# A LoRA update on one core: the first eight tiles as two parts, their stores behind VectorE's turn

## The chip, the cores and the metric

The kernel runs on one core of one Trainium2 chip. The metric is device time in microseconds of one execution; three executions of the kernel before gave a median of 123.61 us, from 123.61 to 123.78. The core has TensorE (PE in the profile), VectorE (DVE), ScalarE (ACT), GpSimd (POOL) and SyncE (SP). SyncE does no arithmetic; here it issues all transfers. They run on 16 DMA engines, which serve one queue.

## The reference

```python
batch, seq, d_model, r = 16, 512, 768, 16     # x: 16 x 512 x 768, all float32
lora = np.matmul(np.matmul(x, A), B)          # A: 768 x 16, B: 16 x 768
return (x + scale * lora).astype(np.float32)  # scale = 0.5
```

There are 8192 rows of x. About 25 MB are read and 25 MB written; the two products are small beside that.

## The kernel before, in words

**Tiles and parts.** A tile is 128 rows by 768 columns, 3,072 bytes on each of the 128 partitions of the on-chip memory; x is 64 tiles. `PARTS` (line 14) cuts them into stretches of rows. Within a part of S tiles, partition p holds S consecutive rows of x, so a transfer of the whole part reads or writes S x 3,072 bytes in one go on each partition. A transfer of only some of a part's tiles (`memory`, line 96) touches a piece of each of these stretches and steps over the rest. The buffer `x_sb` has room for all parts but the last; the last 16 tiles go into the slots of the first 16, once those are stored.

**Loads and stores.** `LOADS` (line 106) and `STORES` (line 128) list transfers as (part, first tile, tiles). Before the change the first part has 8 tiles. It is loaded as 2 and then 6 tiles, and stored as one transfer of 8. Each load has a semaphore of its own; the first two stores have `s_out0` and `s_out1`. A transfer's semaphore is full at 16.

**Groups.** Compute goes by 8 groups of 8 tiles. For each group ScalarE and GpSimd cast x to half precision (`narrowed`, line 186), VectorE transposes in blocks of 32 (`turned`, line 248), TensorE multiplies with A (`projected`, line 278) into `ps_yt`, ScalarE scales and spreads the result into `y_bd` (line 238), TensorE multiplies with B in four pairs of tiles (`raised`, line 293) into two PSUM buffers `lora_ps`, and VectorE adds each pair to x in place (`summed`, line 252). VectorE turns group g+1 before it adds group g.

**Order.** Every engine's program is written out by hand, with waits on semaphores. SyncE's (`on_sync`, line 135) is what the change touches most. It issues the first two loads, the small ones of A and B, four more loads, then waits: for the sums of groups 0 and 1 (line 144, where it also tells TensorE that a PSUM buffer is free), and then for `s_lora` to reach 10, which is TensorE's second pair of group 2 (line 169). Then it issues the stores of parts 0 and 1. When the first has landed it issues the first half of the last load, when the second has landed the second half. The three stores of 16 tiles follow, each when its groups are summed; the first of these also waits for `s_raise`, TensorE's start of group 5's product with B.

Of the kernel before, what the change touches and what calls it, by code (L numbers as in the profile page):

```python
# [10 lines left out]

PARTS = [8, 8, 16, 16, 16]


GROUP = 8
# [11 lines left out]
def kernel(  # L29
# [8 lines left out]
    nc = tc.nc  # L38
# [9 lines left out]
    NC = D // 64  # L48
    NG = sum(PARTS) // GROUP
    PAIRS = GROUP // 2  # L50
    assert sum(PARTS) * P == T and NG * GROUP == sum(PARTS)
    sc = float(scale)


    def sb(name, shape, dtype):
        return nc.alloc_sbuf_tensor(name, shape, dtype).ap()
# [3 lines left out]

    ROOM = sum(PARTS[:-1])
    x_all = sb("x_sb", [P, ROOM, D], fp32)
# [20 lines left out]
    def sem(name):  # L83
        sems.append(nc.alloc_semaphore(name))
        return sems[-1]
# [4 lines left out]
    tok = 0  # L90
    for i, S in enumerate(PARTS):
        parts.append(tok)
# [3 lines left out]
    def memory(t2, i, s, n):  # L96
        S = PARTS[i]
        return t2[ds(parts[i], S * P), :].rearrange("(p s) d -> p s d", s=S)[:, ds(s, n), :]

    def held(i, s, n):  # L100
        return tiles(where.index((i, s)), n)

    def tiles(t, n):
        return x_all[:, ds(t % ROOM, n), :]

    LOADS = [
        (0, 0, 2), (0, 2, 6), (1, 0, 8), (2, 0, 8), (2, 8, 8), (3, 0, 16), (4, 0, 8), (4, 8, 8)
    ]
    s_load = [sem(f"s_load{k}") for k in range(len(LOADS))]

# [8 lines left out]
    s_first, s_narrow, s_turned, s_taken = sem("s_first"), sem("s_narrow"), sem("s_turned"), sem("s_taken")  # L119
    s_y, s_spread, s_lora = sem("s_y"), sem("s_spread"), sem("s_lora")  # L120

    s_free = [sem(f"s_free{p}") for p in range(PAIRS)]
    s_out0, s_out1, s_raise = sem("s_out0"), sem("s_out1"), sem("s_raise")

    s_sum, s_out = sem("s_sum"), sem("s_out")

    MMS = 2 * NC
    STORES = [(0, 0, 8), (1, 0, 8), (2, 0, 16), (3, 0, 16), (4, 0, 16)]

    STORED = [where.index((i, s + n - 1)) // GROUP for i, s, n in STORES]  # L130

    section = ExitStack()
    section.enter_context(tc.tile_critical(no_gpsimd_drain=True))  # L133

    def on_sync(e):
        def load(k):
            ld = LOADS[k]
            e.dma_start(out=held(*ld), in_=memory(x2, *ld)).then_inc(s_load[k], 16)  # L138

        def summed(k):  # L140
            e.wait_ge(s_sum, k + 1)
            if STORED[k] + 1 < NG:

                e.sem_inc(s_free[PAIRS - 1], 1)

        def store(k, done):
            st = STORES[k]
            e.dma_start(out=memory(out2, *st), in_=held(*st)).then_inc(done, 16)

        load(0)  # L150
        load(1)
        e.wait_ge(s_ready, 1)
        blocks = A.rearrange("(c e) r -> c (e r)", e=64)
        for c in range(SETS):
            e.dma_start(
                out=a_rows[c : SET * SET : SET, :], in_=blocks[ds(c * SET, SET), :]
            ).then_inc(s_a, 16)
        e.wait_ge(s_brows, 1)
        e.dma_start(out=b_rows[0 : R * APART : APART, :], in_=B).then_inc(s_b, 16)
        for k in range(2, len(LOADS) - 2):  # L160
            load(k)

        for p in range(2, PAIRS):
            e.sem_inc(s_free[p], 1)
        summed(0)
        summed(1)


        e.wait_ge(s_lora, 2 * PAIRS + 2)
        store(0, s_out0)  # L170
        store(1, s_out1)
        e.wait_ge(s_out0, 16)
        load(len(LOADS) - 2)
        e.wait_ge(s_out1, 16)
        load(len(LOADS) - 1)
        for k in range(2, len(STORES)):
            summed(k)
            if k == 2:


                e.wait_ge(s_raise, 6)
            store(k, s_out)

    here = set()

# [55 lines left out]
    def on_vector(e):  # L241
        e.wait_ge(s_a, SETS * 16 + 1)
        e.transpose(  # L243
            out=a_t[0:Q].rearrange("i k r c -> i (k r) c"),
            in_=a_rows[0:Q].rearrange("c (i k r) -> c (k r) i", k=2, r=R),
        ).then_inc(s_ready, 1)

        def turned(first, n):
            ts = [v[:, ds(first, n), :].bitcast(fp32) for v in (xt, xn)]
            return e.transpose(out=ts[0], in_=ts[1])  # L250

        def summed(g, p):
            xs = tiles(g * GROUP + 2 * p, 2)
            e.wait_ge(s_lora, g * PAIRS + p + 1)
            ins = e.tensor_tensor(out=xs, in0=xs, in1=lora[p % 2], op=mybir.AluOpType.add)  # L255
            if p + 1 == PAIRS and g in STORED:
                ins.then_inc(s_sum, 1)
            elif g + 1 < NG or p + 2 < PAIRS:
                ins.then_inc(s_free[p], 1)

        for h in range(2):
            e.wait_ge(s_first, h + 1)
            ins = turned(h * SUB, SUB)
        ins.then_inc(s_turned, 1)
        for g in range(NG):
            if g + 1 < NG:
                e.wait_ge(s_y, g + 1)
                e.wait_ge(s_narrow, 2 * (g + 1))  # L268
                turned(0, GROUP).then_inc(s_turned, 1)
            for p in range(PAIRS):  # L270
                summed(g, p)

    def on_tensor(e):
# [58 lines left out]
        for p in range(PAIRS):  # L332
            raised(p)

    on_sync(nc.sync)
    on_gpsimd(nc.gpsimd)
    on_scalar(nc.scalar)
    on_vector(nc.vector)
    on_tensor(nc.tensor)

    nums = [s.num for s in sems]
    assert nums == list(range(nums[0], nums[0] + len(nums))) and sems[-2:] == [s_sum, s_out]

    nc.gpsimd.wait_ge(s_sum, len(STORED))
    nc.gpsimd.sem_clear(range(nums[0], s_sum.num))
    nc.gpsimd.wait_ge(s_out, (len(STORES) - 2) * 16)
    nc.gpsimd.sem_clear(range(s_sum.num, s_out.num + 1))
    section.close()

# [34 lines left out]
```

## Time and profile before

| What | Value |
| --- | --- |
| median of three runs | 123.61 us (123.61 to 123.78) |
| profiled execution, its own time | 123.76 us |
| its span, first to last instruction | 121.9 us |
| DMA queue busy | 96.8% of 16 engines' span |
| moved | 50.43 MB, mean 414 GB/s |
| VectorE busy | 81.7 us, 67% |
| TensorE, ScalarE, GpSimd busy | 41%, 31%, 23% |

The profile's page gives each engine's busy time and share of the span. Its groups of instructions have the line, the engine, the operation, what it writes and reads, the count, the busy time in us, the mean ns of one, then the idle time of the engine just before them and what ended it. The chain lists, from the last instruction backwards, what released what. A line of a timeline or of the chain begins with its start and its duration in us. SyncE's lines (SPq) show the time at which a transfer is issued, not when it moves; a timeline merges issues of one line into one entry from the first to the last. Besides these the trace has a record of every DMA packet with its start, duration and size; a packet here is one partition's row of a transfer, and each DMA engine takes 8 of the 128 rows. Packets of one engine follow each other without a break, so 16 series can be followed from start to end.

### The profile page before, as it was taken

What the parts mean: (1) busy time and instruction counts of PE and PEld (TensorE: products, weight loads), DVE (VectorE), ACT (ScalarE), POOL (GpSimd) and SP (SyncE); (2) the same over time, 40 slices, a digit from 0 to 9 for tenths busy, and PEclk for the clock granted to TensorE, in tenths of its full rate; (3) what the DMA queues carried; (4) which work ended last, traced back from release to release, by engine and by line L of the source; (5) the groups of instructions that cost most, each with busy time, mean ns of one, the idle gap of its engine ahead of it and who ended that gap; (6) DMA issues with size and microseconds to landing.
All of it is one profiled execution on the core that took longest, in us unless ns stands there. A gap on an engine that the chain in (4) does not pass through costs nothing.

```text
span 121.9 us, 885 instructions
## 1 busy us (share of the span) xinstructions
PE 50.5 (41%) x322; PEld 29.3 (24%) x322; DVE 81.7 (67%) x42; ACT 37.4 (31%) x43; POOL 28.4 (23%) x24
## 2 busy tenths in 40 slices
PE   0000239487457457647756714774674320000000
PEld 0000026244233233424424402442442110000000
DVE  0003850799999999999999959999995991000000
ACT  4003929444426402917230093643004000000000
POOL 7732638044026002607100090630000000000000
PEclk9999999999999999999999999999999985555555
DMA  3999999999997996999989999998998999899890
GB/s 67 421 429 429 443 443 403 451 435 419 476 516 339 435 516 298 460 403 443 443 363 460 427 427 468 451 484 387 419 500 387 403 516 403 371 516 419 355 516 0
DMA packets 1928, 50.43 MB, mean 414 GB/s; under 512 B 236, under 2 KB 236, under 8 KB 392
## 3 DMA queue, kind: packets, MB, share of 16 engines
q1 hardware_dynamic: 1928, 50.43, 96.8%
HBM read 25.26 MB, written 25.17 MB: 414 GB/s over the span
## 4 chain that ended last, share of the span: by engine, by line
DVE 33%; DMA 29%; PE 9%; ACT 6%; POOL 2%; issue 2%; SPq 0%; DVEq 0%
DVE x_sb L255 21%; DMA x_sb<-in_x_dram 20%; DVE xt L250 12%; DMA out_dram<-x_sb 9%; PE ps_yt L281 6%; ACT xn L194 3%; PE lora_ps L302 3%; ACT y_bd L238 2%; POOL xn L194 2%; SPq L138 0%; SPq L379 0%; DVEq L268 0%; SPq L133 0%
## 5 line engine op out<-in xcount | busy, mean ns | idle before, releaser
L255 DVE TENSOR_TENSOR x_sb<-x_sb,lora_ps 128x1536 f32<-128x1536 f32 x32 | 53.7, 1735 | 1.4 <-PE lora_ps L302 1.4
L302 PE MATMUL lora_ps<-b_mm,y_bd 128*128 128x512 f16 (+1 forms) x128 | 25.1, 328 | 23.7 <-ACT y_bd L238 15.3
L194 ACT CAST xn<-x_sb 128x3072 f16<-128x3072 f32 (+1 forms) x9 | 23.4, 2609 | 37.2 <-DMA x_sb<-in_x_dram 28.0
L250 DVE STREAM_TRANSPOSE xt<-xn 128x3072 f32<-128x3072 f32 (+1 forms) x9 | 27.0, 3005 | 6.7 <-PE ps_yt L281 4.9
L194 POOL CAST xn<-x_sb 128x3072 f16<-128x3072 f32 (+1 forms) x8 | 20.7, 2588 | 45.3 <-DMA x_sb<-in_x_dram 28.6
L281 PE MATMUL ps_yt<-xt,w_bd 128*128 128x256 f16 x192 | 25.7, 285 | 11.9 <-DVE xt L250 11.9
L281 PEld LDWEIGHTS ps_yt<-xt,w_bd 128*128 128x128 f16 x192 | 18.7, 100 | 19.6 <-issue 15.0
L302 PEld LDWEIGHTS lora_ps<-b_mm,y_bd 128*128 128x128 f16 x128 | 10.5, 97 | 36.8 <-ACT y_bd L238 17.5
L238 ACT ACTIVATE y_bd<-ps_yt 32x256 f16<-32x256 f32 x32 | 12.0, 374 | 17.7 <-PE ps_yt L281 17.4
L243 DVE STREAM_TRANSPOSE a_t<-a_rows 32x1024 f32<-32x1024 f32 x1 | 1.9, 1945 | 11.2 <-DMA a_rows<-in_A_dram 11.2
L315 PE MATMUL lora_ps<-b_half,pick 128*128 128x512 f16 (+1 forms) x2 | 0.8, 500 | 12.5 <-POOL b_half L212 12.5
L315 PEld LDWEIGHTS lora_ps<-b_half,pick 128*128 128x128 f16 x2 | 0.1, 105 | 12.5 <-issue 12.5
L220 POOL COPY w_bd<-w_one 32x384 f16<-32x384 f16 x4 | 2.0, 501 | 0.2
L212 POOL CAST b_half<-b_rows 128x768 f16<-128x768 f32 x1 | 0.8, 830 | 4.5 <-DMA b_rows<-in_B_dram 4.5
L194 ACT ACT_TABLE_LOAD x1 | 1.3, 1283 | 0.9 <-SPq L133 0.9
L202 POOL MEMSET w_bd<- 128x1536 f32 x1 | 1.4, 1372 | 0.0
L199 POOL MEMSET a_rows<- 32x1024 f32 x1 | 0.9, 941 | 0.5 <-SPq L133 0.5
L214 POOL CAST w_one<-a_t 32x384 f16<-32x384 f32 x1 | 0.8, 847 | 0.9 <-DVE a_t L243 0.9
L231 ACT CAST b_mm<-lora_ps 128x768 f16<-128x768 f32 x1 | 0.8, 798 | 0.0
L200 POOL MEMSET b_rows<- 128x768 f32 x1 | 0.7, 727 | 0.0
L203 POOL MEMSET y_bd<- 128x512 f32 x1 | 0.5, 514 | 0.0
L205 POOL TENSOR_SCALAR_AFFINE_SELECT pick<-pick 128x128 f16<-128x128 f16 x1 | 0.3, 300 | 0.0
(5 smaller groups left out, 0.6 us busy)
## 6 DMA issues: line engine op xcount, KB each, us to landing
out_dram<-x_sb SPq DMA_DIRECT2D x3, 6144.0 KB, 20.0
x_sb<-in_x_dram SPq DMA_DIRECT2D x5, 3072.0 KB, 14.8
x_sb<-in_x_dram SPq DMA_DIRECT2D x1, 6144.0 KB, 41.9
out_dram<-x_sb SPq DMA_DIRECT2D x2, 3072.0 KB, 14.9
x_sb<-in_x_dram SPq DMA_DIRECT2D x1, 2304.0 KB, 9.7
x_sb<-in_x_dram SPq DMA_DIRECT2D x1, 768.0 KB, 4.5
a_rows<-in_A_dram SPq DMA_DIRECT2D x3, 16.0 KB
b_rows<-in_B_dram SPq DMA_DIRECT2D x1, 48.0 KB, 7.4
```

The source lines that it names most:

```text
L194: ins = copy(out=xn[:, ds(first, n), :], in_=tiles(t, n))
L199: e.memset(a_rows[0:Q], 0.0).then_inc(s_ready, 1)
L202: e.memset(w_bd.rearrange("p c k m -> p (c k m)").bitcast(fp32), 0.0)
L212: e.tensor_copy(out=b_half, in_=b_rows).then_inc(s_bh, 1)
L220: e.tensor_copy(out=w_bd[ds(b * Q, Q), :, :, ds(b * Q, R)], in_=w_one).then_inc(s_w, 1)
L238: last = e.mul(out=y_bd[q, :, q], in_=y_ps[q, :, :], mul=sc)
L243: e.transpose(out=a_t[0:Q].rearrange("i k r c -> i (k r) c"), in_=a_rows[0:Q].rearrange("c (i k r) -> c (k r) i", k=2, r=R),).then_inc(s_r ...
L250: return e.transpose(out=ts[0], in_=ts[1])
L255: ins = e.tensor_tensor(out=xs, in0=xs, in1=lora[p % 2], op=mybir.AluOpType.add)
L281: mm = e.matmul(y_ps, w_bd[:, c, k, :], xv[:, :, c, :, k], start=(m == 0), stop=(m == MMS - 1),)
L302: mms.append(e.matmul(t[:, k, ds(n0, w)], y_bd[:, 2 * p + k, :], b_mm[:, ds(n0, w)], start=True, stop=True,))
L315: last = e.matmul(lora[0][:, 0, ds(n0, w)], pick.rearrange("p b r -> p (b r)"), b_half[:, ds(n0, w)], start=True, stop=True,)
```

## The change

The first part of 8 tiles becomes two parts, of 2 and of 6 tiles. The two loads stay as large as they were and in the same order, but each now reads one run of memory. The store of 8 tiles becomes two stores, first that of the 6 tiles, then that of the 2, both counted by `s_out0`; the load into these 8 slots waits for both (32 instead of 16). VectorE's turn of group 3 is cut into one instruction of 7 tiles and one of 1, and the first of these raises a new semaphore, `s_most`. SyncE's wait ahead of the first stores is for `s_most` instead of `s_lora`. The list `STORED`, which says behind which group a store comes, keeps its five entries.

```diff
-PARTS = [8, 8, 16, 16, 16]
+PARTS = [2, 6, 8, 16, 16, 16]
...
-        (0, 0, 2), (0, 2, 6), (1, 0, 8), (2, 0, 8), (2, 8, 8), (3, 0, 16), (4, 0, 8), (4, 8, 8)
+        (0, 0, 2), (1, 0, 6), (2, 0, 8), (3, 0, 8), (3, 8, 8), (4, 0, 16), (5, 0, 8), (5, 8, 8)
...
-    STORES = [(0, 0, 8), (1, 0, 8), (2, 0, 16), (3, 0, 16), (4, 0, 16)]
+    STORES = [(1, 0, 6), (0, 0, 2), (2, 0, 8), (3, 0, 16), (4, 0, 16), (5, 0, 16)]
...
+    assert STORED[0] == STORED[1]
+    STORED = STORED[1:]
...
-        e.wait_ge(s_lora, 2 * PAIRS + 2)
+        e.wait_ge(s_most, 1)
         store(0, s_out0)
-        store(1, s_out1)
-        e.wait_ge(s_out0, 16)
+        store(1, s_out0)
+        store(2, s_out1)
+        e.wait_ge(s_out0, 32)
         load(len(LOADS) - 2)
         e.wait_ge(s_out1, 16)
         load(len(LOADS) - 1)
-        for k in range(2, len(STORES)):
+        for k in range(2, len(STORED)):
             summed(k)
...
-            store(k, s_out)
+            store(k + 1, s_out)
...
-                turned(0, GROUP).then_inc(s_turned, 1)
+                if g == 2:
+                    turned(0, GROUP - 1).then_inc(s_most, 1)
+                    turned(GROUP - 1, 1).then_inc(s_turned, 1)
+                else:
+                    turned(0, GROUP).then_inc(s_turned, 1)
...
-    nc.gpsimd.wait_ge(s_out, (len(STORES) - 2) * 16)
+    nc.gpsimd.wait_ge(s_out, (len(STORES) - 3) * 16)
```

More of the change, by code (lines that the diff above doesn't have):

```diff
@@ L123 @@
     s_out0, s_out1, s_raise = sem("s_out0"), sem("s_out1"), sem("s_raise")
+    s_most = sem("s_most")
     s_sum, s_out = sem("s_sum"), sem("s_out")
     MMS = 2 * NC
-    STORES = [(0, 0, 8), (1, 0, 8), (2, 0, 16), (3, 0, 16), (4, 0, 16)]
+    STORES = [(1, 0, 6), (0, 0, 2), (2, 0, 8), (3, 0, 16), (4, 0, 16), (5, 0, 16)]
     STORED = [where.index((i, s + n - 1)) // GROUP for i, s, n in STORES]
+    assert STORED[0] == STORED[1]
+    STORED = STORED[1:]
     section = ExitStack()
```

## The prediction

> **What bounds the kernel now.** I read the page's engine table first, then its DMA rows, the idle columns of the groups, the chain in order of time, SyncE's timeline and VectorE's. The page:
>
> ```profile
> PE 50.5 (41%) x322; PEld 29.3 (24%) x322; DVE 81.7 (67%) x42; ACT 37.4 (31%) x43; POOL 28.4 (23%) x24
> DMA packets 1928, 50.43 MB, mean 414 GB/s; under 512 B 236, under 2 KB 236, under 8 KB 392
> q1 hardware_dynamic: 1928, 50.43, 96.8%
> L194 ACT CAST xn<-x_sb 128x3072 f16<-128x3072 f32 (+1 forms) x9 | 23.4, 2609 | 37.2 <-DMA x_sb<-in_x_dram 28.0
> L250 DVE STREAM_TRANSPOSE xt<-xn 128x3072 f32<-128x3072 f32 (+1 forms) x9 | 27.0, 3005 | 6.7 <-PE ps_yt L281 4.9
> ```
>
> One DMA queue is busy 96.8% of the span; no compute engine is above 67%. The kernel is the time that 16 DMA engines need for 50.43 MB. The chain shows this late, because it follows instructions:
>
> ```profile
> 43.92 11.36 DMA out_dram<-x_sb
> 55.30 14.76 DMA x_sb<-in_x_dram
> 70.11 2.76 POOL xn L194
> 72.97 3.38 DVE xt L250
> 94.27 6.75 DVE x_sb L255 x4
> ```
>
> The reader is to see that the transfers here take longer than their bytes: 11.36 us for a 3 MB store, 14.76 for a 3 MB load. The packet records explain it. The queue is served in order: the first store runs behind what is left of the 6 MB load, and the next load behind the second store. In the steady part a 24,576-byte row takes 912 ns on one engine (eight of them 7.3 us, which is also the distance between the ends of consecutive 3 MB loads), a 49,152-byte row 1815, an 18,432-byte row 686, a 6,144-byte row 234. These lie on one line, 904 ns per 24,576 bytes and about 8 ns for each row. From the first data packet at 1.99 us to the last at 120.5 hardly an engine waits for descriptors. VectorE's and SyncE's lists show the place that is edited:
>
> ```profile
> 41.84 3.36 DVE L250 STREAM_TRANSPOSE xt<-xn 128x3072 f32<-128x3072 f32 x1
> 45.12 6.71 DVE L255 TENSOR_TENSOR x_sb<-x_sb,lora_ps 128x1536 f32<-128x1536 f32 x4
> ```
>
> ```profile
> 0.97 0.85 SPq L138 DMA_DIRECT2D x_sb<-in_x_dram  x2
> 43.92 0.82 SPq L148 DMA_DIRECT2D out_dram<-x_sb  x2
> 55.30 7.74 SPq L138 DMA_DIRECT2D x_sb<-in_x_dram  x2
> 74.87 26.51 SPq L148 DMA_DIRECT2D out_dram<-x_sb  x3
> ```
>
> The first store is issued at 43.92, while the 6 MB load ends on the first DMA engine at 47.0 and on the last at 48.0. The last store is issued at 101.0, though the store before it leaves the first engine only at 105.4: the end of compute has 4.4 us to spare. So only three things can move the time: work added to the queue, a gap in it, and stalls of single packets. The end is set by the slowest of the 16 engines (about 120.55 by its packets; the fastest is through at 119.5).
>
> Stalls in the packet records, above the steady price: the 128 rows of the first load take 310 ns on average instead of 234 (0.6 us an engine; single rows up to 1114); four rows of the 6 MB load that start at 45.0 to 45.4 are 65 to 466 ns late; rows of the second store that start at 60.2 to 62.2 are late on seven engines, by 250 to 1060 ns an engine. The four engines that end last, 120.3 to 120.55, all have the last kind and lost 0.4 to 1.2 us in the first load as well.
>
> **The change part by part.** Sums are against the profiled execution, 123.76 us (span 121.9 and 1.86 around it). It lies 0.15 above the median of 123.61, so I carry differences over to the median.
>
> *Rows of the first store.* Eight rows of 912 become eight of 686 and eight of 234 on each engine: 7.36 against 7.30, and one more completion packet of 9 ns. +0.07 us, in the full queue, so on the path. The loads keep their row sizes: 0. The prices of 6,144-byte rows are those of reads; no such row is written before. Bound for the writes: 234 from the steady rows, 310 from the first load's mean, that is +0.07 to +0.68. I take 234, because these stores stand in the middle of a full queue, like the steady rows.
>
> *Another DMA on the queue.* Loads queued one behind the other land 7.31 us apart, 8 rows of 914, so one more transfer in a full queue has no price of its own: 0. (The Trainium skill, "DMA: Bandwidth & Descriptors", Anatomy of one DMA, gives each transfer a fixed cost of about 2.0 us, mostly completion. By that rule the sum would be 2 us higher; the rows above show none of it while the queue is full.)
>
> *The later issue.* The old wait ended at 43.92 with TensorE's second pair of group 2. The new one ends with seven tiles of VectorE's turn for group 3. Four tiles take 1.751 us and eight 3.363, so 0.403 a tile and 0.139 fixed: seven take 2.96, from 41.84 to 44.80. The stores are issued 0.9 later, at about 44.82, 45.2 and 45.6 (332 to 425 ns each). The first issue of the kernel, at 0.97, has its first packet at 1.99, 1.0 us on; so store rows are there at 45.9, 1.1 us before the first engine runs out. The 6 tiles then keep each engine 5.5 us, the second and third issue are far ahead of need. No gap: 0. If the lead were gone, each us of lateness would cost an engine 1 us.
>
> *What stands behind the waits on SyncE.* Behind the new wait stand only the three stores. The load of group 6 waits for 32 instead of 16, that is for both first stores: 55.28+0.07. It is queued behind the 7.3 us of the third store, so 0. The last load follows the third store's landing, 62.68+0.07, and SyncE's relay of the free PSUM buffer (line 144) comes after that; TensorE waited 0.5 us for it, and VectorE takes that pair only at 66.65, over 2 us after TensorE has it. 0.
>
> *VectorE.* A second instruction of 0.139 us fixed delays group 3 by 0.14. VectorE waits 1.3 us for GpSimd's cast at 72.97 (the load of group 6), which swallows it; without that cover the 4.4 us before the last store would. 0.
>
> *Where the first load reads.* Its rows of 6,144 bytes lay 24,576 apart; now they are one run. Bounds: all 0.6 us an engine of stalls go, or as much is added. The nearest rows are the later 3 MB loads, each one run, with stalls of 7 ns a row; but they stand in a full queue, and part of the first rows' 800 ns is the first answer of memory, which stays. I take a third: -0.2.
>
> *Stalls at the two changes of direction.* Reads to writes (45.0 to 47.7): at the kernel's other such place, 76.4, the store was issued at 74.87, 1.5 us before the first engine was through with reading, and no row there is over 60 ns late. The first store is issued 3.1 us ahead and has four; it will be issued 2.2 ahead. Writes to reads (60.2 to 63): seven engines, and the load there is issued over 6 us ahead, as it will be. Which engines lose depends on how far they are apart, and that comes from the first load and from the stalls at 45. Bounds: -0.85 (the slowest engine loses its 0.85 there no more, and ends like the fastest) to +0.5 (one more stall of the 45 us kind on it). I take -0.25, half a stall of 0.45 to 0.47, since the lead moves about half of the way to the undisturbed case.
>
> Sum: +0.07 -0.2 -0.25 = -0.38: 123.38 by the profiled execution, 123.23 by the median, put at 123.25.
>
> **The rivals.** What a measurement of this kernel can tell from no change is about 0.2%, 0.25 us.
>
> *Nothing but rows (0.29).* The stalls stay as they are and the time is 123.61+0.07 = 123.68; with stalls dealt out differently, 123.4 to 123.85. For it: the bytes and the full queue do not change. Against: a tail of a us between the first and the last engine, all of it from places that the edit touches.
>
> *Small rows written slowly (0.18).* If the 6,144-byte rows cost in the store what they cost on average in the first load, 310, each engine loses 8 x 76 ns = 0.6 us more: 123.61+0.07+0.61 = 124.3. It decides from about 256 ns a row, where 0.07 and 8 x 22 ns make 0.25. For it: no such row was written before, and half the rows at the kernel's start were late. Against: those late rows are at the start, the later ones of the same load are at 234 throughout.
>
> *Descriptors too late (0.05).* If an issue into this queue needs 3 us instead of 1.0, the first engine stands from 47.0 to 47.8: up to 0.8, 124.4. Against it speaks 74.87, where a lead of 1.5 us was enough.
>
> *The first load slower as one run (0.02).* As many stalls again, +0.6: 124.3.
>
> *A price for each transfer (0.01).* 2 us for the one more transfer give 125.6; the rows show none (the page of the Trainium skill named above has it).
>
> **How the numbers follow.** The forecast, faster by stalls that go, has 0.45, at 123.25, from 122.75 (-0.85 at the turn, 0.07 for rows, rounded) to 123.35. Within 0.2%: 0.29. Slower: 0.18+0.05+0.02+0.01 = 0.26. I leave 0.05 of the fast side below 122.75 and the dearest 0.1 of the slow side above 124.2, so the range is 122.75 to 124.2.
>
> **What would show it.** In the new profile the first three stores start at 44.8, and the DMA share stays at 97%. Right: the first load's landing before 5.5 us (GpSimd's first cast begins at 5.57 now), the span below 121.7, no rise in mean ns of the other groups. Wrong: a cast of group 0's last six tiles later than 11.10, a first pair of stores that takes over 7.5 us in the queue, or a gap between 47 and 48. The forecast fails if the stalls belong to memory itself and not to the lead and the spread, for then only the +0.07 is left.

## The result, and the profile after

The changed kernel takes 124.32 us (median of 16 runs, 123.53 to 125.53), the kernel before 123.71 us beside it (16 runs, 123.30 to 123.96). The ratio is 1.0046, with a 95% interval of 1.0029 to 1.0063: slower by about 0.6 us, where the forecast was faster by 0.4. The run of 125.53 us counts as a slow one, and slow runs are left out of all ratios and means here. A second measurement, on another chip, gave 1.0015 (0.9994 to 1.0037); where the two differ is told below, and why they do stays open.

The page of the changed kernel shows the queue as full as before, and the same compute:

```profile
span 121.7 us, 887 instructions
DMA packets 2072, 50.43 MB, mean 415 GB/s; under 512 B 252, under 2 KB 252, under 8 KB 536
q1 hardware_dynamic: 2072, 50.43, 97.1%
L255 DVE STREAM_TRANSPOSE xt<-xn 128x3072 f32<-128x3072 f32 (+3 forms) x10 | 27.2, 2725 | 6.8 <-PE ps_yt L290 4.5
```

The span is 121.7, a little under the 121.9 of before, though this execution's own time is 124.09 against 123.76. So 2.39 us lie around the span instead of 1.86, and the loss of this execution is wholly there. No row of the groups can show it. What does show something is the DMA view of the time after the last instruction (window 119 to 126 us), which has a queue that is not there before the change. First its lines after the change, then the line of before, with one packet fewer:

```profile
DMA packets 17, 0.01 MB, mean 1 GB/s; under 512 B 16, under 2 KB 16, under 8 KB 16
q14 instruction: 1, 0.01, 0.5%
```

```profile
DMA packets 16, 0.00 MB, mean 0 GB/s; under 512 B 16, under 2 KB 16, under 8 KB 16
```

One fetch of 8,192 bytes of instructions starts at 123.8 us, 2.1 us after the last instruction of the span. The trace of before has such fetches only ahead of its first instruction.

Inside the span, lines from the timelines of SyncE, of VectorE from 40 us on, and of all engines from 5 to 12 us (this one after, then before); each line has start, duration, engine and instruction:

```profile
44.16 2.10 SPq L152 DMA_DIRECT2D out_dram<-x_sb  x3
55.46 7.61 SPq L142 DMA_DIRECT2D x_sb<-in_x_dram  x2
74.80 26.55 SPq L152 DMA_DIRECT2D out_dram<-x_sb  x3
```

```profile
41.17 3.43 DVE L255 STREAM_TRANSPOSE xt<-xn 128x2688 f32<-128x2688 f32 x2
```

```profile
5.35 1.46 POOL L199 CAST xn<-x_sb 128x1536 f16<-128x1536 f32 x1 [0.51 <-DMA x_sb<-in_x_dram]
10.90 1.47 ACT L199 CAST xn<-x_sb 128x1536 f16<-128x1536 f32 x1 [8.70 <-DMA x_sb<-in_x_dram]
```

```profile
5.57 1.46 POOL L194 CAST xn<-x_sb 128x1536 f16<-128x1536 f32 x1 [0.73 <-DMA x_sb<-in_x_dram]
11.10 1.47 ACT L194 CAST xn<-x_sb 128x1536 f16<-128x1536 f32 x1 [8.91 <-DMA x_sb<-in_x_dram]
```

The casts that follow the first two loads start at 5.35 and 10.90; before, at 5.57 and 11.10. The first load did get quicker by 0.2 us. The stores are issued at 44.16 and not at the 44.8 of the forecast, because VectorE reached its turn of group 3 at 41.17, 0.67 earlier than in the profile of before.

### The profile page after: what moved, and what is told of

Same layout as the page of the kernel before. It is cut to its first block, busy times and chain, and to the rows that moved or that the text cites. A ratio compares the mean times of both kernels' runs of the same rounds, so it can differ in the third digit from the quotient of the medians.

```text
span 121.7 us, 887 instructions
## 1 busy us (share of the span) xinstructions
PE 51.4 (42%) x322; PEld 29.9 (25%) x322; DVE 81.9 (67%) x43; ACT 37.5 (31%) x43; POOL 28.4 (23%) x24
## 4 chain that ended last, share of the span: by engine, by line
DVE 38%; DMA 29%; PE 6%; ACT 5%; issue 2%; POOL 2%; SPq 1%; DVEq 0%
DVE x_sb L260 23%; DMA x_sb<-in_x_dram 20%; DVE xt L255 15%; DMA out_dram<-x_sb 9%; PE ps_yt L290 5%; ACT xn L199 3%; POOL xn L199 2%; PE lora_ps L311 1%; ACT y_bd L243 1%; SPq L142 0%; SPq L152 0%; SPq L388 0%; DVEq L273 0%; SPq L137 0%
## 5 line engine op out<-in xcount | busy, mean ns | idle before, releaser
L311 PE MATMUL lora_ps<-b_mm,y_bd 128*128 128x512 f16 (+1 forms) x128 | 26.1, 337 | 24.9 <-ACT y_bd L243 16.6
L255 DVE STREAM_TRANSPOSE xt<-xn 128x3072 f32<-128x3072 f32 (+3 forms) x10 | 27.2, 2725 | 6.8 <-PE ps_yt L290 4.5
```

Source lines behind the costliest of these rows:

```text
L311: mms.append(e.matmul(t[:, k, ds(n0, w)], y_bd[:, 2 * p + k, :], b_mm[:, ds(n0, w)], start=True, stop=True,))
```

## The experiments

The number around the span is a run's time less its span; spans are on record to 0.1 us, so each such number is good to 0.05. Unless something else is said, "stalls" are what the rows of a stretch took above their steady price (234, 686, 912 or 1815 ns), summed over the packet records of a profile and divided by 16 engines.

**Which half of the change costs.** First the kernel before again, then each half alone, then the cut of the turn with nothing that uses it.

> The kernel before, unchanged, so that the span and the time around the span of many of its executions are known. Theory 'end of the program': the changed kernel's time outside its span is 1.9 us in some executions and 2.4 in others, and its trace has a fetch of 8,192 bytes at 123.8 us, 2.1 us after its last instruction, that the trace of before lacks; then here the time outside the span is 1.9 in all executions, and no such fetch is seen. Theory 'packet stalls': the time outside varies here in the same way, and the spans are shorter by the whole 0.5 us than the changed kernel's 122.05 (median), that is about 121.5. Ratio 1.000 within 0.0015.

Measured: 0.9999 (0.9990 to 1.0008). Spans 121.7 to 122.1, 1.76 to 1.86 us around them, no late fetch. The kernel before ran beside every experiment; up to the 16th, 96 of its executions on four chips have a mean span of 121.79, none over 122.0, and at most 1.87 around it. One of the eleven measured here has a span of 122.1, and two of the 17 beside the last two experiments have 122.1 and 122.2.

> The two parts and their stores (6 tiles first) with the old wait for TensorE and the turn uncut. Theory 'rows': 8 ns a row and one transfer, +0.07 us, ratio 1.0006. Theory 'packet stalls': the stalls at 45 and 60 us follow the spread of the DMA engines, so this alone gives most of the loss, ratio 1.003 to 1.005, with spans of 121.6 to 122.6. Theory 'end of the program' gives 0.25 us (half of the executions 0.5 longer outside the span) if it is SyncE's program, with one more transfer, that grew too long, and 0 if it is VectorE's.

```diff
-PARTS = [8, 8, 16, 16, 16]
+PARTS = [2, 6, 8, 16, 16, 16]
...
-    STORES = [(0, 0, 8), (1, 0, 8), (2, 0, 16), (3, 0, 16), (4, 0, 16)]
+    STORES = [(1, 0, 6), (0, 0, 2), (2, 0, 8), (3, 0, 16), (4, 0, 16), (5, 0, 16)]
```

The loads and the calls of the stores are as in the change. Measured: 1.0021 (1.0006 to 1.0036), 1.77 to 1.86 around the span: SyncE's longer program costs nothing there. The spans fall in two groups, six at 121.6 to 121.8 and six at 122.2 to 122.5.

> The old part of 8 tiles with its one store, with the new wait and the cut turn. Theory 'packet stalls': the store is issued 0.9 us later; if the lead matters, the rows that start at 45.0 to 45.4 lose less, ratio 0.998 to 1.000. Theory 'end of the program': 2.4 us outside the span in half of the executions, ratio 1.002, if it is VectorE's program that grew too long; 1.9 in all if it is SyncE's. Theory 'rows': 1.000.

```diff
-        e.wait_ge(s_lora, 2 * PAIRS + 2)
+        e.wait_ge(s_most, 1)
...
-                turned(0, GROUP).then_inc(s_turned, 1)
+                if g == 2:
+                    turned(0, GROUP - 1).then_inc(s_most, 1)
+                    turned(GROUP - 1, 1).then_inc(s_turned, 1)
+                else:
+                    turned(0, GROUP).then_inc(s_turned, 1)
```

Measured: 1.0050 (1.0031 to 1.0068); 2.31 to 2.38 us around the span in five of six executions, 1.95 in the other; the profile of one with 2.38 has the late fetch.

> Only VectorE's turn of group 3 is cut in 7 and 1 tiles; the stores wait as before. Theory 'end of the program', VectorE's case: 1.9 or 2.4 us outside the span, ratio 1.002, and a late fetch in the trace; in SyncE's case 1.9 and 1.000. Theories 'packet stalls' and 'rows': 1.000, span as before.

```diff
-                turned(0, GROUP).then_inc(s_turned, 1)
+                if g == 2:
+                    turned(0, GROUP - 1)
+                    turned(GROUP - 1, 1).then_inc(s_turned, 1)
+                else:
+                    turned(0, GROUP).then_inc(s_turned, 1)
```

Measured: 1.0040 (1.0026 to 1.0053), mean span 121.82 as before the change, and 1.90, 1.92, 2.31, 2.37 and 2.43 around it. The profiled one is a 1.90, and has no late fetch. A cut that nobody waits for costs nearly all that the whole change did in the first measurement, and none of it inside the span.

**One VectorE instruction fewer, one more, eight more.** In the first of these GpSimd waits once for TensorE's product in VectorE's place, so that VectorE's separate wait goes and its program is as long as before the change (57 VectorE records in the trace, as before; the changed kernel, the cut alone and the one small write have 58).

> The changed kernel with one instruction fewer on VectorE: for group 6 GpSimd's cast waits for TensorE's whole product of group 5, so VectorE needs no wait of its own for it, and its program is as long as before the change. Theory 'length of VectorE's program': the time outside the span goes back to 1.8 us in all executions and no fetch follows the end; the span stays 122.0 (median), so the ratio falls from 1.0046 to 1.0015-1.002. Rival 'cut turn': the price is the cut's own (two instructions, or the stores' wait on them), then 1.9 or 2.4 us outside the span stay and the ratio stays 1.004-1.005.

```diff
+            if g == 6 and first == SUB:
+                e.wait_ge(s_y, g)
+            else:
+                e.wait_ge(s_taken, g)
...
-                e.wait_ge(s_y, g + 1)
+                if g != 5:
+                    e.wait_ge(s_y, g + 1)
```

Measured: 1.0011 (0.9990 to 1.0033), median 123.47 against 123.56; 1.79 to 1.86 around the span in all twelve.

> The kernel before with one more instruction on VectorE, a write of 32 bytes a partition at the start, where VectorE is idle until 11 us. Theory 'length of VectorE's program': 1.9 or 2.4 us outside the span, ratio 1.003-1.004, as for the cut turn, and the span stays 121.8. Rival 'cut turn': 1.8 and 1.000.

```diff
     def on_vector(e):
+        e.memset(spare, 0.0)
```

Measured: 1.0052 (1.0039 to 1.0065); the mean span is the same as before (121.76), and 2.40 to 2.44 lie around it in all five. The DMA view of the end has the instruction queue again:

```profile
q14 instruction: 1, 0.01, 0.4%
```

> Eight small writes more on VectorE at the start instead of one. Theory 'a step, not a price for each': 2.3 to 2.5 us outside the span as with one, ratio 1.004-1.006. Rival 'a price for each instruction': 0.6 us for the first means 4 us and more for eight, ratio over 1.03.

The write stands eight times, into eight columns of the same spare buffer. Measured: 1.0033 (1.0021 to 1.0045). Not as expected in its place: 1.78 to 1.86 around the span, but spans of 122.1 to 122.3 beside 121.7 to 122.0 for the kernel before. In its profile all engines go through the closing barrier, and VectorE's step in it is late by 0.4 us:

```
closing step (DRAIN), start in us:   SyncE 121.28   ScalarE 121.29   TensorE 121.35   VectorE 121.71 (135 ns)
the same with one small write more:  SyncE 121.30   ScalarE 121.31   TensorE 121.37   VectorE 121.33 (10 ns)
```

The fetch is there too, but earlier: at 122.38 us, 0.3 us after the last instruction instead of 2.1.

```profile
q14 instruction: 1, 0.01, 0.3%
```

So with seven instructions more, both the fetch and the lost time come earlier, and the time is now lost inside the span. This fits a VectorE that runs out of fetched instructions at the end of its program, but it does not show it: the late step starts 0.67 us ahead of the fetch's record. It is a step and no price for each instruction: eight cost no more than one.

Then the changed kernel and the one with an instruction fewer again, unaltered, on one chip.

> The changed kernel on the chip of the next run, so that the two can be set side by side. Theory 'length of VectorE's program': 1.9 to 2.45 us outside the span in every execution, most of them near 2.4; span 121.6 to 122.6; ratio 1.004-1.005. If the first measurement was an accident of its chip, 1.8 and 1.000-1.002.

> The changed kernel with one VectorE instruction fewer, a second time. Theory 'length of VectorE's program': 1.8 us outside the span throughout, ratio 0.999-1.002, and at least 0.3 us below the changed kernel of the same call, while the spans of the two agree within 0.2. Rival 'cut turn': as the changed kernel.

Measured: the changed kernel 1.0015 (0.9994 to 1.0037), with one instruction fewer 1.0011 (0.9994 to 1.0027). Around the span 1.86 to 1.96 for the first, 1.77 to 1.86 for the second. The expectation of 2.4 and of 0.3 us between the two missed. With the longer program an execution has either about 1.9 or about 2.4 around its span, and on this chip all twelve had the first. The profiles go with that: a late fetch in those with 2.38 and more (the changed kernel, the wait alone, one small write), none in those with 1.90 and 1.96 (the cut alone, this one), and none in those with 1.8 but the eight writes with their earlier fetch. With 58 records, 13 of 16 executions of the wait alone, the cut alone and the one write, on two other chips, had about 2.4, and 8 of 15 of the first measurement. What decides between the two, the chip or something else, is open.

**The layout.** What is left is the span: 122.05 on average in the first measurement against 121.79.

> The old part of 8 tiles, loaded as before, but stored as 6 and then 2 tiles, each with steps in memory; old wait, turn uncut. The two new parts alone gave spans of 121.6-121.8 and of 122.2-122.5, median 122.0 against 121.8. Theory 'two stores': this comes from the shorter rows of the stores, and is here again, ratio 1.001-1.003, with spans up to 122.5. Rival 'layout': it comes from where the parts lie in memory, and here the ratio is 1.0005, the 0.07 us of the rows.

```diff
-    STORES = [(0, 0, 8), (1, 0, 8), (2, 0, 16), (3, 0, 16), (4, 0, 16)]
+    STORES = [(0, 2, 6), (0, 0, 2), (1, 0, 8), (2, 0, 16), (3, 0, 16), (4, 0, 16)]
```

SyncE's calls of the three first stores are as in the change. Measured: 1.0012 (1.0003 to 1.0021), mean span 121.86 beside 121.76, none over 122.0. Shorter rows and one more store cost 0.1 us, about the 0.07 worked out. The long spans belong to the layout.

The next table is worked out from the packet records: mean stalls in ns an engine over the profiles named.

```
rows that start at (us)                                    1.5-5.6  5.6-44  44-47  59-64  64-78
old layout (before, again, cut, write, wait, two stores)       654     135     30    118     41
new layout (after, parts, one less twice, again)               360     207     87    341      8
```

The new layout saves 0.29 us an engine in the first load. It has 0.07 more while the loads run, 0.06 more at the change from reading to writing (44 to 47 us) and 0.22 more at the change from writing to reading (59 to 64 us). What the first load gains is given back. All five profiles of the new layout here fell on executions with spans of 121.5 to 121.8, so they show none of the long ones.

**The lead of a store.** The lead is the time from a transfer's issue to the end of the first DMA engine that is still busy in the other direction. Does it matter at such a change of direction? One kernel issues the first stores later, on TensorE's second product of group 3, without a new VectorE instruction; one without SyncE's wait at all.

> The kernel before, with the first stores waiting for TensorE's second product of group 3 (about 45.5 us instead of 43.9), without a new instruction on VectorE. Theory 'the later issue costs': the late wait with the cut turn had a median span of 122.0 against 121.8 with the cut turn alone; then here 122.0 or more and a ratio of 1.002. Rival 'the later issue helps or is nothing': 121.6 to 121.8, ratio 0.999-1.000, 1.8 us outside the span in each case.

```diff
-        e.wait_ge(s_lora, 2 * PAIRS + 2)
+        e.wait_ge(s_taken, 4)
```

> The kernel before without SyncE's wait for TensorE: the first stores are issued as soon as group 1 is summed, at about 41.95 us, 5 us before the first DMA engine has read its part of the 6 MB load. Theory 'lead': the sum of stalls of the rows that start from 44 to 47 us, which was 75 and 187 ns an engine with issues at 43.92 and 44.16, and 11 to 22 from 44.5 on, grows to 200 or more, at 42 to 47 us, and the time by 0.2 to 0.5 us, ratio 1.002-1.004. Rival 'chance': the stalls there have nothing to do with the lead, ratio 1.000.

```diff
-        e.wait_ge(s_lora, 2 * PAIRS + 2)
```

SyncE's first store line in the two profiles, the later first, then the early one:

```profile
46.48 0.82 SPq L148 DMA_DIRECT2D out_dram<-x_sb  x2
```

```profile
41.68 0.82 SPq L148 DMA_DIRECT2D out_dram<-x_sb  x2
```

Measured: 1.0067 (1.0044 to 1.0090) for the later, 1.0037 (1.0024 to 1.0050) for the early one, both from the span. With the issue at 46.48 the engines are done reading from 46.5 on, and the first rows of the store come 0.85 us and more after the issue: 12 of 16 engines stand idle for 0.24 to 0.93 us near 47, and at 59 to 64 us the stalls are 963 ns. At 41.68 all 16 engines stall in the last rows of the 6 MB load, 600 ns an engine, and hardly at 59 to 64 (8 ns). The windows 41 to 48 and 59 to 64 (bytes by the start of their rows, in GB/s at the end of a line) show it, of the early store first, then of the kernel before:

```profile
41.00:48.00 7.00, 3.79 (x24) 2.09 (x24) 7.00 (x4) 1.01 (x3) 0.00 (x0) 1.00 0.99 383
59.00:64.00 5.00, 2.58 (x20) 1.49 (x18) 5.00 (x3) 1.50 (x4) 0.00 (x0) 1.00 1.03 442
```

```profile
41.00:48.00 7.00, 3.79 (x24) 2.09 (x24) 7.00 (x4) 1.33 (x4) 0.00 (x0) 1.00 0.98 418
59.00:64.00 5.00, 3.28 (x22) 1.69 (x20) 5.00 (x3) 1.50 (x4) 0.00 (x0) 1.00 0.97 393
```

All 20 profiles in order of the first store's issue (the same program differs by up to 0.7 us from one execution to the next):

```
issued at, us            41.68  43.59  43.76  43.78  43.92  44.06  44.16  44.20  44.34  44.34
stalls at 44-47, ns        600    543    304    327     75     39    187    195     22     12
issued at, us            44.40  44.45  44.50  44.56  44.64  44.74  44.88  45.02  45.26  46.48
stalls at 44-47, ns        108    110     20     12     16     11     11     18     10      4
```

In these profiles rows that are being read stall when a store has been issued long before its turn: over 300 ns with an issue by 43.8, 3.2 us and more ahead of the first engine's end (its landing, about 47.0), and 20 or less from 44.5 on. In between the new layout has more than the old (108 to 195 against 12 to 75). There its first engine ends earlier, at 46.6 to 46.9, so that the four issues from 44.16 to 44.45 have leads of 2.2 to 2.6 us; the old layout has 11 to 22 ns with leads of 2.4 to 2.7. So the lead alone does not set the stalls. The price of too little lead is a gap.

**The change from writing to reading, and the order.** If a lead over 3 us is what hurts, the load of group 6, issued 7 us ahead, should gain from a later issue.

> The changed kernel with one VectorE instruction fewer, and the load of group 6 issued only after TensorE's last pair of group 3 (about 59.0 us instead of 55). Theory 'lead at the second turn': the stalls of rows that start from 59 to 64 us, 266 to 441 ns an engine in this layout, fall below 100, as those at 45 us did with a later store; spans of 121.2 to 121.6, none above 122, ratio 0.996-0.999. Rival 'layout': they stay at 250-450 and so do spans up to 122.5, ratio 1.001.

```diff
+        e.wait_ge(s_lora, 4 * PAIRS)
         load(len(LOADS) - 2)
```

The same line in the kernel before, and in the two parts with the old wait:

> The kernel before with the same later load (about 59.2 us). Theory 'lead at the second turn': its stalls there, 77 to 272 ns an engine, fall too, ratio 0.998-1.000. Rival 'layout': nothing changes, 1.000.

> The two parts with the old wait and the uncut turn, and the later load. Theory 'lead at the second turn': spans without the group at 122.2-122.5 that the two parts alone had, ratio 0.998-1.000 instead of 1.002. Rival 'layout': 1.002, two groups of spans.

Measured: 1.0054 (1.0033 to 1.0075), 1.0103 (1.0086 to 1.0120) and 1.0044 (1.0026 to 1.0063). The theory fell: all three are slower, and the stalls at 59 to 64 us do not fall with the new wait as a rule (630, 37 and 134 ns, with first stores at 45.26, 43.76 and 43.59). They may depend on what happened at 44 to 47 us: 8 ns follow 600 there, and 963 follow 4. But it is no rule: in the old layout 11 to 40 ns are followed by 77 to 110, and 75 by 272. In the first of the three the landings of that load lie 1.94 us apart, the next store's issue at 76.18 follows the last of them by 5.0, and 14 of 16 engines stand idle for 0.2 to 1.0 us at 76 us. Why the second is the slowest its profile does not tell, as it fell on the shortest of its executions (122.0; the others 122.7 to 123.2).

Then the two parts with the old wait and the other order, `STORES = [(0, 0, 2), (1, 0, 6), ...]`:

> The two parts with the old wait, the 2 tiles stored before the 6. Theory 'order of the stores': the stalls at 59-64 us come from the small store that stands just ahead of the next one, and fall below 120, spans 121.5-121.8, ratio 0.999-1.000. Rival 'layout': as with the 6 first, 220 or more, ratio 1.002.

Measured: 1.0022 (1.0006 to 1.0038), spans 121.6 to 122.5, 191 ns at 59 to 64 and 327 at 44 to 47. The same as with the 6 tiles first; the order of the two stores isn't the cause.

Last, the first store of 16 tiles earlier, in the changed kernel with one instruction fewer and in the kernel before:

> The changed kernel with one VectorE instruction fewer, and its first 16-tile store issued after the casts of group 6 (about 72.9 us instead of 74.8). Theory 'the third store comes too late': that store follows the last engine's landing of the load of group 6 by 4.8 to 5.0 us and its first row comes 0.85 us and more later, while the first engine is done with reading 7.3 us after its own landing; so it stands idle where the landings lie over 1.4 us apart, as at 76 us in the run with the late load (1.94 apart). The new layout's profiles have 0.9 to 1.35, the old one's 0.5 to 1.0, so only the new one has long executions. Then here no span over 122.1, median 121.5 to 121.7, ratio 0.997-1.000. Rival 'stalls alone': the slowest engine's stalls make the long executions, and spans up to 122.5 stay in a third of them, ratio 1.001.

```diff
-                e.wait_ge(s_raise, 6)
+                e.wait_ge(s_narrow, 12)
```

> The kernel before with the same earlier store. Theory 'the third store comes too late': the old layout has no such executions, so nothing is gained: 0.9995-1.0005 if the longer lead (3.1 us ahead of the first engine, as at 43.92) has no stalls, up to 1.001 with the 75 ns an engine seen there. Rival 'stalls alone': the same.

Measured: 1.0099 (1.0074 to 1.0124) for the changed kernel, 1.0011 (0.9999 to 1.0023) for the one before, whose spans now reach 122.6. This theory fell too, on the other side: with the earlier issue,

```profile
72.93 28.54 SPq L152 DMA_DIRECT2D out_dram<-x_sb  x3
```

the reads of the last load stall by 495 ns an engine at 64 to 78 us (215 in the other kernel, issued at 73.14), where profiles with 74.5 to 75.3 have 60 or less. No engine stands idle there. It looks like the lead of the first stores once more, at another place (3.4 to 3.5 us here), and it shows what the wait for `s_raise` is worth in the changed kernel. What makes the long executions of the new layout stays open. No version here beats the kernel before; of those with the new layout the nearest is the one with one VectorE instruction fewer, level with it.

## Why the prediction was wrong

Two steps failed: VectorE's cut, put at 0, cost 0.1 or 0.6 us around the span, and the stalls at the changes of direction, put at -0.25, grew. Point by point, by its own steps:

- *Rows of the first store*, +0.07: right. Two stores in the old layout cost 0.1 us of span.
- *Another DMA on the queue*, 0: right, and the 2 us that the Trainium skill's page gives were not seen; its section describes transfers that GpSimd issues, and here SyncE issues them.
- *The later issue*, no gap: right for the place that it took, but it came at 44.16 in the profile and 44.45 to 45.02 in others, not at 44.82, since the compute ahead of it differs between executions by as much. The 1.1 us to spare were about right: 1.7 us later there is a gap.
- *VectorE*, "A second instruction of 0.139 us fixed delays group 3 by 0.14", swallowed, 0: **this step failed.** The 0.14 is swallowed. But the instruction makes VectorE's program longer, and that costs 0.1 or 0.6 us around the span, where no row of a timeline stands: 2.17 us on average in the first measurement against 1.81 in the 96 executions of the kernel before, +0.36 of its +0.6; in the second measurement +0.1. One small write at the start of VectorE's program does the same; taking an instruction out undoes it. That it is the late fetch which costs the time is argued, not shown. The forecast counted the time around the span as a constant, 1.86.
- *Where the first load reads*, -0.2: right, -0.29 an engine, and 0.2 us at the casts.
- *Stalls at the two changes of direction*, -0.25: **this step failed too, in sign.** Both places together have 148 ns an engine in the old layout and 428 in the new, +0.28 by the means of the table, and 347 and 573 in the two profiles compared first. The first half of the reasoning held: stalls at 45 us fall with a shorter lead, to 18 ns or less from 44.7 on. But there were only 30 to 75 ns to win there in the old layout, and at 60 us the profile of before, with 272 ns, was the worst of its kind; in the new layout that place took 0.22 more, for which no cause was found. Summed with the first load's gain, nothing is left. The rest, +0.26 us of span in the first measurement (+0.06 in the second), comes mostly from executions of 122.2 us and more, 4 of 15 and 4 of 12, while the 96 of the kernel before end at 122.0; their cause is open.
- *The range*: its lower end doesn't follow as written, since 123.61 - 0.85 + 0.07 is 122.83 and not 122.75. Nothing hangs on it.

Of the rivals none was either of these. "Nothing but rows" describes the span of most executions (8 of 15 and 8 of 12 are at 122.0 or less); the slow writes are out, as two stores in the old layout show, and so is the first load that gets slower.

## What to carry to other kernels

Where a queue of transfers is full from start to end, small edits are paid where no engine's row shows it: look at the run's time less its span, and at fetches of instructions after the last one, before the groups. An instruction more on one engine cost 0.1 or 0.6 us once, around the span, and an instruction taken out elsewhere on that engine took it back. At a change from loads to stores try an issue some 1.5 to 1.9 us before the first DMA engine runs dry: in these profiles such leads had stalls of 60 ns or less in both layouts, 2.2 to 2.6 us had up to 195 in one of them, over 3 us had 39 to 600, and 0.3 and 0.6 left gaps. A stall saved at one place of a full queue is not yet a gain: sum it over all the changes of direction, in several profiles of each kernel.

## What was not expected of the hardware

- A fetch of 8,192 bytes of instructions behind the end of the span, together with 0.5 to 0.6 us more around it; with seven more instructions the fetch came 0.3 us behind the end, and 0.4 us were lost at VectorE's last step but one, inside the span. The Trainium skill, "Runtime: NRT & Kernel Launch", Instruction fetch mechanics, says that crossing a block of instructions is mostly hidden. No trace here has such a fetch between its first and its last instruction, so none tests that; behind the last one it stands in those four profiles that lost 0.4 us or more at their end.
- Rows in flight of a load took up to 0.9 us longer (1815 ns plus 934) where a store had been issued 3 to 6 us ahead of the first engine's end, though both use one queue in order.
- The issue of one store changed the stalls at both changes of direction, 15 us apart: 600 and then 8 ns with the early issue, 4 and then 963 with the late one. Between these extremes there is no rule (75 and 272; 11 and 85).
